# The bonus sums of an RWKV time mixing, tied to four steps of a block inverse's substitution

## The chip, the cores and the metric

The kernel runs on one core of a Trainium2 chip. A core has five engines that run side by side, each with its own fixed, in-order list of instructions: TensorE (PE, matmuls), VectorE (DVE), ScalarE (ACT), GpSimd (POOL) and SyncE (SP, which here only starts transfers). They wait for one another through semaphores. Transfers between the chip's memory (DRAM, HBM) and the core's buffers are issued from SP's, ACT's and POOL's lists and carried out by 16 DMA engines. The metric is device time in microseconds.

## The reference

One block of a streaming encoder, 512 frames of width 1024, in float32. A common in-projection feeds an RWKV-7 time mixing (8 heads of 64), a gated linear recurrence, and sigmoid gates that merge the two; then come a cross-attention into 256 memory frames and a gated convolutional feed-forward layer. What matters here:

```python
y = rwkv7_recurrence(r, decay, k, v, -kk, kk * a)
mean = jnp.mean(y, axis=-1, keepdims=True)
var = jnp.mean(jnp.square(y - mean), axis=-1, keepdims=True)
y = ((y - mean) * lax.rsqrt(var + LNX_EPS)).reshape(bsz, s, A_WIDTH) * lnx_g + lnx_b
bonus = jnp.sum(r * k * r_k, axis=-1, keepdims=True) * v
return (y + bonus.reshape(bsz, s, A_WIDTH)) * g
```

The bonus is a sum over a head's 64 channels for every frame, times v. It depends on r, k and v alone, and is needed only where y is normalised.

## The kernel before

**Layout.** Channels lie on the 128 partitions and frames along the free axis. A tile of 128x512 therefore holds two heads ("a pair", j = 0 to 3) for all frames. Matmuls keep float32 accuracy by splitting a float32 operand in a rounded high part (an ACT cast) and the remainder (a DVE subtraction), and summing two or three products. The sum over a head's channels, `sum_exact`, is such a product with a block matrix of ones: ACT casts the high part (L154), DVE makes the low part (L155), PE multiplies both (L156, L157).

**In-projection.** 38 column blocks of 24 matmuls each (three products, L160 to L162, by eight row blocks) go to the `in_ps` accumulators. Their weights are streamed: SP loads `win_r` (L102, four buffers), ACT casts it to `win_h` (L114), DVE makes `win_l` (L115); high and low parts have three buffers.

**Time mixing.** The pairs' stage lies between column blocks of the in-projection: `prep` and `prep2` build decays and scaled keys (tiles `AK`, `KBt`), with `ss` sums (also `sum_exact`) in between; `scores` does 16 small matmuls (L605), which DVE masks and evacuates to `BZ` and `AK` (L609, L610), and SP stores a part of `BZ` to DRAM, `dM` (L612). Then `bonus(j)` runs: DVE multiplies r, r_k and k (L586, tile `pr`), `sum_exact` sums them to `bo`, DVE multiplies by v (L589), ACT adds the bias (L590), and ACT's queue stores the result to DRAM, `dBo[j]` (L591).

**Block inverse.** All pairs' small matrices are loaded back from `dM` in one layout, `Nm` (L654, SP's queue). DVE inverts 128 triangular 32x32 blocks (two for each of 64 chunks of a head, one on each partition) by substitution: from s = 30 down to 0 a product (L660, tile `zz`) of (31-s) x (31-s) elements and a reduction (L661, tile `Zt`) of 31-s, so that the steps grow. The step s = 20 has an 11-element result. PE does gate blocks of the in-projection meanwhile, and ACT their sigmoids (L237, tile `gs`). The inverse goes through DRAM to `ZA`, the products `zh` and `zo` (L687, L695) use it, then come the chunk recurrence and `group_norm`, which loads `dBo` again (L821).

**What sets the order.** A scheduler fixes each engine's list when the kernel is built. The code's order counts unless a line has priority (weights, and the loads around the inverse) or is tied: `tc.issue_after(x)` puts what is inside it behind instruction x.

Of the kernel before, what the change touches and what calls it, by code (L numbers as in the profile page):

```python
# [9 lines left out]
F32 = mybir.dt.float32  # L10
F32R = mybir.dt.float32r
AF = mybir.ActivationFunctionType
ALU = mybir.AluOpType
AX = mybir.AxisListType
# [3 lines left out]
P = 128  # L18
T = 512
# [6 lines left out]
NPAIR = NH // 2  # L26
# [27 lines left out]
def hybrid_block_kernel(ctx: ExitStack, tc: tile.TileContext, xT_d, mT_d, pv_d, cst_d, win_d, wk_d, wv_d,  # L54
                        lup_d, gup_d, rga_d, rgx_d, wba_d, wbb_d, wmix_d, wq_d, wo_d, wfi_d, wfo_d, out_d):
    nc = tc.nc
    V, S, PE = nc.vector, nc.scalar, nc.tensor
# [12 lines left out]
    def mm_ps(name):  # L70
        return pmm.tile([P, T], F32, tag="mm", name=name)

    def rw_ps(name, pool=None, tag="rw", **kw):
        return (pool or prw).tile([P, T], F32, tag=tag, name=name, **kw)
# [9 lines left out]
    def par(name, i, n=1):  # L84
        o = PV[name][0]
        return pv[:, o + i:o + i + n]
# [63 lines left out]
    def sum_exact(ps, blocks, src, pool, tag, name):  # L150

        hi = pool.tile(list(src.shape), F32R, tag=tag, name=f"{name}_h", bufs=2)
        lo = pool.tile(list(src.shape), F32R, tag=tag, name=f"{name}_l", bufs=2)
        S.copy(hi, src)  # L154
        V.tensor_tensor(lo, src, hi.bitcast(F32), ALU.subtract)  # L155
        PE.matmul(ps, blocks, hi, start=True, stop=False)  # L156
        PE.matmul(ps, blocks, lo, start=False, stop=True)  # L157
# [36 lines left out]
    bonesr = cp.tile([P, P], F32R, name="bonesr")  # L194
# [72 lines left out]
    with tc.tile_pool(name="p0", bufs=1, reuse_waits="tile") as p0:  # L267
# [36 lines left out]
        for m in range(KB):  # L304
            ps = rw_ps(f"k_ps{m}") if 3 <= m < 6 else mm_ps(f"k_ps{m}")
# [93 lines left out]
    dBo = dr.tile([4, P, T], F32, name="dBo")  # L399
# [82 lines left out]
    vT = pa.tile([P, NPAIR, T], F32, name="vT")  # L482
# [4 lines left out]
    tp = tp_ctx.enter_context(tc.tile_pool(name="tp", bufs=1, reuse_waits="tile"))  # L487
# [28 lines left out]
    def inproj(i):  # L516
        ps = mm_ps(f"in_ps{i}")
        dense(ps, uin, lambda kb: (h2[:, 0, kb, :], h2[:, 1, kb, :]), KB, NSUM.get(i, 0))
        return ps

    def evac_shift(ps, blk, out):
        q = pp.tile([P, T], F32, tag="q", name=f"q{blk}", bufs=2)
        V.tensor_copy(q[:, 0:1], qb[:, blk:blk + 1])
        S.activation(q[:, 1:T], ps[:, 0:T - 1], AF.Identity, scale=par("mu", blk), bias=par("b_in", blk))
        V.scalar_tensor_tensor(out, ps, omu[:, blk:blk + 1], q, ALU.mult, ALU.add)  # L525
# [17 lines left out]
    def prep(j):  # L543
        sl = slice(j * P, (j + 1) * P)
        psw, psa = rw_ps(f"psw{j}"), rw_ps(f"psa{j}")
        for i, ps in enumerate((psw, psa)):
            PE.matmul(ps, lhi[:, i, sl], pwa[i], start=True, stop=False)
            PE.matmul(ps, llo[i][:, sl], pwa[i], start=False, stop=True)
        L = pp.tile([P, T], F32, tag="L", name=f"L{j}")
        tab(L, psw, AF.Sigmoid, bias=par("w0", j))  # L550
        at = pp.tile([P, T], F32, tag="at", name=f"at{j}")
        tab(at, psa, AF.Sigmoid, bias=par("a0", j))
        V.tensor_tensor_scan(L, smask, L, 0.0, ALU.mult, ALU.add)
        Pp = pp.tile([P, NC, HD + 1], F32, tag="Pp", name=f"Pp{j}")
        V.memset(Pp[:, :, 0:1], 1.0)
        tab(Pp[:, :, 1:], L.rearrange("p (c t) -> p c t", t=HD), AF.Exp, scale=-C0)
        tab(L, L, AF.Exp, scale=C0)
        V.tensor_copy(PC[:, j, :], Pp[:, :, HD])
        return at, L, Pp
# [22 lines left out]
            hs = half[e]  # L582
            V.tensor_tensor(AK[hs, e, jc, HD:P], c3(pr)[hs], Pp[hs, :, 1:], ALU.mult)

    def bonus(j, pk, pr):
        V.scalar_tensor_tensor(pr, pr, par("r_k", j), pk, ALU.mult, ALU.mult)  # L586
        ps = rw_ps(f"bo{j}")
        sum_exact(ps, bonesr, pr, tp, "xb", f"bo{j}")
        V.tensor_tensor(pr, ps, vT[:, j, :], ALU.mult)  # L589
        S.activation(pr, pr, AF.Identity, bias=par("lnx_b", j))  # L590
        nc.scalar.dma_start(dBo[j], pr)  # L591

# [3 lines left out]
    def scores(j):  # L598
        for e in range(2):
            hs, oh = half[e], half[1 - e]  # L600
            for cg in range(2):
                ps = rw_ps(f"sc{j}_{e}_{cg}")
                i0 = j * NC + cg * 4
                for i in range(4):
                    PE.matmul(ps[:, i * P:(i + 1) * P], kb_cols(j, e, cg * 4 + i), AK[hs, e, i0 + i, :],  # L605
                              start=True, stop=True)
                p3 = ps.rearrange("p (c t) -> p c t", t=P)
                m3 = scmask.unsqueeze(1).to_broadcast([P, 4, P])
                V.tensor_tensor(BZ[hs, i0:i0 + 4, :], p3[hs], m3[hs], ALU.mult)  # L609
                V.tensor_tensor(AK[oh, e, i0:i0 + 4, :], p3[oh], m3[oh], ALU.mult)  # L610
            with tc.high_priority(offset=1000000):
                nc.sync.dma_start(dM[e * 32 + j * NC:e * 32 + (j + 1) * NC].rearrange("i s t -> s i t"),  # L612
                                  BZ[hs, j * NC:(j + 1) * NC, 0:HD])

    def gate_block(b):
        ps = inproj(22 + b)
        sg = tp.tile([P, T], F32, tag="st", name=f"gs{b}", bufs=2)
        tab(sg, ps, AF.Sigmoid, bias=par("b_in", 22 + b))
        nc.scalar.dma_start(dG[b], sg)

    for jp in range(2):
        js = (2 * jp, 2 * jp + 1)
        pks, prs = {}, {}
        for j in js:
            pks[j] = pp.tile([P, T], F32, tag="pk", name=f"pk{j}", bufs=2)
            evac_shift(inproj(4 + j), 4 + j, pks[j])
        for j in js:
            prs[j] = pp.tile([P, T], F32, tag="pr", name=f"pr{j}", bufs=3)
            evac_shift(inproj(j), j, prs[j])
        for j in js:  # L630
            evac_shift(inproj(8 + j), 8 + j, vT[:, j, :])
        for j in js:
            if j == 3:
                for i in IN_REST[:NEARLY]:
                    gate_block(i - 22)
            at, L, Pp = prep(j)
            prep2(j, pks[j], prs[j], at, L, Pp)
            scores(j)
            bonus(j, pks[j], prs[j])

    pp_ctx.close()
    pq_ctx = ExitStack()
    pq = pq_ctx.enter_context(tc.tile_pool(name="pq", bufs=1, reuse_waits="tile"))
    YB = pq.tile([P, 4, T], F32, name="YB")


    with tc.tile_pool(name="pz", bufs=1, reuse_waits="tile") as pz:
        Nm = pz.tile([P, 32, 32], F32, name="Nm")
        Zt = pz.tile([P, 32, 32], F32, name="Zt")
        Zn = pz.tile([P, 32, 32], F32, name="Zn")  # L650
        zz = pz.tile([P, 31 * 31], F32, name="zz")
        with tc.high_priority(offset=1000000):
            for b in range(2):
                nc.sync.dma_start(Nm[b * HD:(b + 1) * HD], dM[:, b * 32:(b + 1) * 32, b * 32:(b + 1) * 32])  # L654
        V.memset(Zt, 0.0)
        V.memset(Zt.rearrange("p a b -> p (a b)")[:, 0:1024:33], 1.0)
        for s in range(30, -1, -1):
            n = 31 - s
            t3 = zz[:, 0:n * n].rearrange("p (a b) -> p a b", b=n)
            V.tensor_tensor(t3, Zt[:, s + 1:, s + 1:], Nm[:, s:s + 1, s + 1:].to_broadcast([P, n, n]), ALU.mult)  # L660
            V.tensor_reduce(Zt[:, s + 1:, s:s + 1], t3, AX.X, ALU.add)  # L661
        V.tensor_copy(Zn, Zt.rearrange("p a b -> p b a"))
        with tc.high_priority(offset=1000000):
            for b in range(2):
                nc.sync.dma_start(dZ[b], Zn[b * HD:(b + 1) * HD])
            nc.sync.dma_start(dZt, Zt[0:HD])
# [197 lines left out]
    def px_scan(b, xb, ga, gx):  # L864
# [5 lines left out]
        V.tensor_tensor(xb, xb, gx, ALU.mult)  # L870
        V.tensor_tensor_scan(YB[:, b, :], ga, xb, 0.0, ALU.mult, ALU.add)

    def py_block(b):
        ps = inproj(18 + b)
        ge = tp.tile([P, T], F32, tag="st", name=f"ge{b}", bufs=2)
        with tc.high_priority():
            tab(ge, ps, AF.Gelu_apprx_tanh, bias=par("b_in", 18 + b))
            V.tensor_tensor(YB[:, b, :], YB[:, b, :], ge, ALU.mult)

# [26 lines left out]
    for b in range(4):  # L906
        yb = YB[:, b, :]
        with tc.high_priority():
# [17 lines left out]
    for m in range(KB):  # L926
        ga = pm.tile([P, T], F32, tag="ga", name=f"gta{m}")
# [26 lines left out]
    for m in range(KB):  # L954
        xin = pm.tile([P, T], F32, tag="xin", name=f"xin{m}")
        nc.scalar.dma_start(xin, xT_d[:, m, :])
        ps = mm_ps(f"mix_ps{m}")
# [23 lines left out]
    pk = pk_ctx.enter_context(tc.tile_pool(name="pk", bufs=1, reuse_waits="tile"))  # L981
# [73 lines left out]
    pr = ctx.enter_context(tc.tile_pool(name="pr", bufs=1, side="right", reuse_waits="tile"))  # L1055
# [17 lines left out]
    for m in order:  # L1073
        ps = mm_ps(f"co_ps{m}")
# [87 lines left out]
    for m0 in range(0, FB, NQ):  # L1162
# [25 lines left out]
        for m in ms:  # L1188
            s = pc.tile([P, T], F32, tag="s", name=f"fs{m}")
# [228 lines left out]
```

## Time and profile before

| | us |
|---|---|
| runs | 909.81, 911.17, 912.35; median 911.17 |
| profiled execution, its own time | 909.73 |
| its span in the profile | 908.0 |
| PE busy | 890.5 (98%) |
| DVE busy | 687.4 (76%) |
| ACT busy | 510.4 (56%) |

The granted clock of PE was 0.998 on average. The profiled execution's span is what its instructions cover; 1.73 us of its time lie around it. A row of a timeline has the start, the duration, engine, line, operation, output and inputs, and in brackets how long the engine had idled just before and what ended it. A row of waits has the waiting instruction, what it waited for, the total in us, how often, and the longest. In the table of stretches the columns are the stretch, its length, and the busy time (and instructions) of PE, PE's weight loads, DVE, ACT and POOL, then the granted clock, the share of the DMA engines and GB/s.

### The profile page before, as it was taken

The numbers are of one execution on the slowest core, as the hardware profiler recorded it, in microseconds if no ns is written. First come the engines' busy times: TensorE is split into PE (matmuls) and PEld (weight loads), VectorE is DVE, ScalarE is ACT, GpSimd is POOL, SyncE is SP. The second block draws the span as 40 slices with busy tenths as digits, with TensorE's granted clock in tenths as the row PEclk, the third lists the DMA queues.
The fourth block names the chain that finished last, engine by engine and source line by source line (L and its number), as shares of the span: only waits on it lengthen the run. The fifth ranks groups of instructions, "written<-read, shape, count | busy, mean of one in ns | idle before, by whom it ended". The sixth has DMA issues, their size and how long they took to land. (4 is left out here: it accounts for less than half of the span.)

```text
span 908.0 us, 15914 instructions
## 1 busy us (share of the span) xinstructions
PE 890.5 (98%) x6218; PEld 776.1 (85%) x6218; DVE 687.4 (76%) x1096; ACT 510.4 (56%) x779; POOL 129.3 (14%) x159
## 2 busy tenths in 40 slices
PE   7999999999999999999999999999999999999996
PEld 6988877788877777887887778999999999999996
DVE  7884598776957585776565568788998888999674
ACT  6674675542236675234454446765665556767663
POOL 0102222010011212001112211111111111201100
PEclk9999999999999999999999999999999999999999
DMA  8878899667499749858788868898989998998963
GB/s 276 277 263 230 186 237 208 179 165 206 139 205 246 167 106 194 258 180 223 210 243 190 177 152 185 240 273 247 280 249 290 258 316 251 248 277 222 269 197 93
DMA packets 102411, 200.07 MB, mean 220 GB/s; under 512 B 25344, under 2 KB 36736, under 8 KB 102272
## 3 DMA queue, kind: packets, MB, share of 16 engines
q1 hardware_dynamic: 69504, 119.75, 41.0%
q0 software_dynamic: 25504, 67.38, 36.8%
q10 hardware_dynamic: 7328, 11.92, 3.9%
q8 instruction: 49, 0.80, 0.3%
q14 instruction: 26, 0.21, 0.1%
HBM read 187.75 MB, written 77.59 MB: 292 GB/s over the span
## 5 line engine op out<-in xcount | busy, mean ns | idle before, releaser
L126 ACT CAST wfi_h<-wfi_r 128x1024 fp32r<-128x1024 f32 x77 | 81.0, 1052 | 76.8 <-PE fx_ps L161 21.1
L160 PE MATMUL in_ps<-hT,win_h 128*128 128x512 f32 x304 | 121.9, 402 | 0.8 <-DVE pr L525 0.7
L162 PE MATMUL in_ps<-hT,win_l 128*128 128x512 f32 x304 | 120.8, 398 | 0.0
L161 PE MATMUL in_ps<-hT,win_h 128*128 128x512 f32 x304 | 120.6, 398 | 0.0
L127 DVE TENSOR_TENSOR wfi_l<-wfi_r,wfi_h 128x1024 fp32r<-128x1024 f32 x77 | 94.0, 1221 | 23.5 <-ACT wfi_h L126 23.3
L425 POOL DMA_DIRECT2D dS<-in_wfi x66 | 66.5, 1044 | 267.0 <-PE in_ps L160 132.4
L114 ACT CAST win_h<-win_r 128x1024 fp32r<-128x1024 f32 x38 | 39.8, 1048 | 71.9 <-PE in_ps L161 70.9
L115 DVE TENSOR_TENSOR win_l<-win_r,win_h 128x1024 fp32r<-128x1024 f32 x38 | 46.4, 1221 | 32.6 <-ACT win_h L114 32.5
L160 PEld LDWEIGHTS in_ps<-hT,win_h 128*128 128x128 f32 x304 | 57.0, 187 | 15.6 <-DVE pr L525 1.1
L161 PEld LDWEIGHTS in_ps<-hT,win_h 128*128 128x128 f32 x304 | 57.0, 188 | 14.0 <-issue 0.7
L162 PEld LDWEIGHTS in_ps<-hT,win_l 128*128 128x128 f32 x304 | 57.0, 187 | 13.9 <-issue 0.2
L461 POOL DMA_DIRECT2D dOs<-in_wfo x54 | 39.9, 804 | 186.0 <-PE fx_ps L160 50.9
L1245 DVE TENSOR_TENSOR wfo_l<-wfo_r,wfo_h 128x1024 fp32r<-128x1024 f32 (+1 forms) x39 | 47.2, 1210 | 13.6 <-ACT wfo_h L1244 13.5
L1244 ACT CAST wfo_h<-wfo_r 128x1024 fp32r<-128x1024 f32 (+1 forms) x39 | 40.4, 1038 | 28.2 <-PE oyz_ps L161 9.8
L161 PE MATMUL fx_ps<-hr,wfi_h 128*128 128x256 f32 x176 | 49.7, 282 | 0.0
L162 PE MATMUL fx_ps<-hr,wfi_l 128*128 128x256 f32 x176 | 49.7, 282 | 0.0
L160 PE MATMUL ox_ps<-go,wfo_h 128*128 128x256 f32 x176 | 49.6, 282 | 0.1
L160 PE MATMUL fyz_ps<-hq,wfi_h 128*128 128x256 f32 x176 | 49.3, 280 | 0.4 <-ACT p L1173 0.4
L160 PE MATMUL fx_ps<-hq,wfi_h 128*128 128x256 f32 x176 | 49.5, 281 | 0.0
L160 PE MATMUL fx_ps<-hr,wfi_h 128*128 128x256 f32 x176 | 49.4, 281 | 0.0
L162 PE MATMUL ox_ps<-go,wfo_l 128*128 128x256 f32 x176 | 49.3, 280 | 0.0
L161 PE MATMUL ox_ps<-go,wfo_h 128*128 128x256 f32 x176 | 49.3, 280 | 0.0
(418 smaller groups left out, 2727.8 us busy)
## 6 DMA issues: line engine op xcount, KB each, us to landing
dS<-in_wfi POOLq DMA_DIRECT2D x66, 512.0 KB, 8.4
wfi_r<-dS SPq DMA_DIRECT2D x44, 512.0 KB, 6.9
win_r<-in_win SPq DMA_DIRECT2D x38, 512.0 KB, 5.0
wfi_r<-in_wfi SPq DMA_DIRECT2D x33, 512.0 KB, 5.6
dS<-dS POOLq DMA_DIRECT2D x22, 512.0 KB, 5.7
dOs<-in_wfo POOLq DMA_DIRECT2D x12, 512.0 KB, 7.8
wv_r<-in_wv SPq DMA_DIRECT2D x8, 512.0 KB, 4.9
dG<-gs ACTq DMA_DIRECT2D x16, 256.0 KB, 2.6
```

What stands on the lines that cost most here:

```text
L114: S.copy(hi[:, o:o + n], raw[:, o:o + n])
L115: V.tensor_tensor(lo[:, o:o + n], raw[:, o:o + n], hi[:, o:o + n].bitcast(F32), ALU.subtract)
L126: S.copy(hi, raw)
L127: V.tensor_tensor(lo, raw, hi.bitcast(F32), ALU.subtract)
L160: first = PE.matmul(ps, lh, rh, start=start, stop=False, **kw)
L161: PE.matmul(ps, lh, rl, start=False, stop=False, **kw)
L162: PE.matmul(ps, ll, rh, start=False, stop=stop, **kw)
L425: return lambda: nc.gpsimd.dma_start(s(out), src, **kw)
L461: yield lambda k=k, w=w, src=src: nc.gpsimd.dma_start(dO[n, m][:, k * P:(k + w) * P], src, **kw)
L1244: S.copy(hi[:, :n], raw[:, :n])
L1245: V.tensor_tensor(lo[:, :n], raw[:, :n], hi[:, :n].bitcast(F32), ALU.subtract)
```

## The change

`bonus` is cut in two. `bonus_terms(j)` stays in the pair's place: it multiplies r, r_k and k and stores that product to DRAM, in `dBo[j]`. Ahead of the substitution four tiles `bt0` to `bt3` are allotted, and ACT's queue loads `dBo[j]` into them. The rest, `bonus(j, bt)`, is written into the substitution's loop and tied behind the reductions of s = 20, 16, 12 and 8 for j = 0, 1, 2 and 3. It overwrites `dBo[j]` with its result, as before. Computation is the same; four stores and four loads of 256 KB are added.

```diff
-    def bonus(j, pk, pr):
+    def bonus_terms(j, pk, pr):
+
         V.scalar_tensor_tensor(pr, pr, par("r_k", j), pk, ALU.mult, ALU.mult)
+        nc.scalar.dma_start(dBo[j], pr)
+
+    def bonus(j, bt):
         ps = rw_ps(f"bo{j}")
-        sum_exact(ps, bonesr, pr, tp, "xb", f"bo{j}")
-        V.tensor_tensor(pr, ps, vT[:, j, :], ALU.mult)
-        S.activation(pr, pr, AF.Identity, bias=par("lnx_b", j))
-        nc.scalar.dma_start(dBo[j], pr)
+        sum_exact(ps, bonesr, bt, tp, "xb", f"bo{j}")
+        V.tensor_tensor(bt, ps, vT[:, j, :], ALU.mult)
+        S.activation(bt, bt, AF.Identity, bias=par("lnx_b", j))
+        nc.scalar.dma_start(dBo[j], bt)
...
             scores(j)
-            bonus(j, pks[j], prs[j])
+            bonus_terms(j, pks[j], prs[j])
...
+    bts = [tp.tile([P, T], F32, tag=("ga", "gx")[j % 2], name=f"bt{j}", bufs=2) for j in range(NPAIR)]
+    for j in range(NPAIR):
+        nc.scalar.dma_start(bts[j], dBo[j])
...
-            V.tensor_reduce(Zt[:, s + 1:, s:s + 1], t3, AX.X, ALU.add)
+            ins = V.tensor_reduce(Zt[:, s + 1:, s:s + 1], t3, AX.X, ALU.add)
+            if s % 4 == 0 and 8 <= s <= 20:
+                with tc.issue_after(ins.ins):
+                    bonus(5 - s // 4, bts[5 - s // 4])
```

In the changed file `bonus_terms` has L587 and L588, the loads of `bt` L651, the substitution L667 and L668, the score evacuations L613 and L614, and the multiply by v L593. `sum_exact` keeps its lines.

**DVE, from the last score evacuation to the substitution.** Before, the bonus of pair 3 (L586, its low part L155, and the multiply by v, L589) lies between the evacuations and the first write of `Zt`:

```order
L610 TENSOR_TENSOR AK_746<-sc3_1_1_1718,cst_76 64x512
L586 SCALAR_TENSOR_TENSOR pr3_1354<-pr3_1354,pv_75,pk3_1278 128x512
L717 SCALAR_TENSOR_TENSOR cst_76<-cst_76 128x128 [waits DVE_49]
L115 TENSOR_TENSOR win_l22_2809<-win_r22_2806,win_h22_2808 128x1024 [waits DMAHW4_49,PE_49,Activation_49]
L155 TENSOR_TENSOR bo3_l_1729<-pr3_1354,bo3_h_1728 128x512 [waits Activation_49]
L589 TENSOR_TENSOR pr3_1354<-bo3_1727,vT_745 128x512 [waits PE_49]
L115 TENSOR_TENSOR win_l23_2843<-win_r23_2840,win_h23_2842 128x1024 [waits DMAHW7_49,PE_49,Activation_49]
L655 MEMSET Zt_1746 128x1024 [waits DMAHW1_49]
```

Now the product of pair 3 (L587) stands ahead of the score evacuations, and the low part of bonus 0 and its multiply stand inside the substitution:

```order
L667 TENSOR_TENSOR zz_1720<-Zt_1718,Nm_1717 128x121 [waits DVE_49]
L115 TENSOR_TENSOR win_l25_2923<-win_r25_2920,win_h25_2922 128x1024 [waits PE_49,Activation_49]
L668 TENSOR_REDUCE Zt_1718<-zz_1720 128x11 [waits DVE_49]
L155 TENSOR_TENSOR bo0_l_1749<-bt0_1706,bo0_h_1748 128x512 [waits DMAHW2_49]
L667 TENSOR_TENSOR zz_1720<-Zt_1718,Nm_1717 128x144 [waits DVE_49]
L668 TENSOR_REDUCE Zt_1718<-zz_1720 128x12 [waits DVE_49]
L667 TENSOR_TENSOR zz_1720<-Zt_1718,Nm_1717 128x169 [waits DVE_49]
L593 TENSOR_TENSOR bt0_1706<-bo0_1747,vT_745 128x512 [waits PE_49]
```

So the low part of bonus 0 comes after the reduction of s = 20, with one weight low part (win_l25) since the substitution's start.

**PE, the bonus products.** Before, both products of pair 3 stand in the column block in_ps28:

```order
L160 MATMUL in_ps28_2735<-hT2_0_89,win_h20_2738 128x512
L156 MATMUL bo3_1727<-bo3_h_1728,bonesr_80 128x512 [waits PE_49,Activation_49]
L161 MATMUL in_ps28_2735<-hT2_1_90,win_h20_2738 128x512
L162 MATMUL in_ps28_2735<-hT2_0_89,win_l20_2739 128x512
L160 MATMUL in_ps28_2735<-hT2_0_89,win_h20_2738 128x512
L161 MATMUL in_ps28_2735<-hT2_1_90,win_h20_2738 128x512
L162 MATMUL in_ps28_2735<-hT2_0_89,win_l20_2739 128x512
L157 MATMUL bo3_1727<-bo3_l_1729,bonesr_80 128x512 [waits DVE_49]
```

Now the first product of bonus 0 stands right behind the score matmuls of pair 3, and the second one 93 rows later, in in_ps31:

```order
L609 MATMUL sc3_1_1_1691<-AK_746,KBt_744 128x128 x3
L156 MATMUL bo0_1747<-bo0_h_1748,bonesr_80 128x512 [waits DVE_49,PE_49,Activation_49]
L160 MATMUL in_ps27_2712<-hT2_0_89,win_h19_2715 128x512
...
L160 MATMUL in_ps31_2851<-hT2_0_89,win_h23_2854 128x512
L161 MATMUL in_ps31_2851<-hT2_1_90,win_h23_2854 128x512
L157 MATMUL bo0_1747<-bo0_l_1749,bonesr_80 128x512 [waits DVE_49]
L162 MATMUL in_ps31_2851<-hT2_0_89,win_l23_2855 128x512
L156 MATMUL bo1_1765<-bo1_h_1766,bonesr_80 128x512 [waits PE_49,Activation_49]
```

Between the scores and L157 of bo0 stand 93 matmuls: the first bonus product, 6 of in_ps27, 72 of in_ps28 to in_ps30, and 14 of in_ps31. The products of bonus 1, 2 and 3 follow, their L157 17, 43 and 81 rows behind that of bonus 0.

**ACT, the cast win_h22 after pair 3's scores.** Before, it stands behind the store of a gate block and no transfer that waits for pair 3:

```order
L114 CAST win_h21_2773<-win_r21_2771 128x1024 [waits DMAHW1_49,PE_49]
L237 ACTIVATE gs4_2697<-in_ps26_2666,pv_75 128x512 [waits DMAHW0_49,PE_49]
L619 DMA dG_712<-gs4_2697 128x512 [waits Activation_49]
L114 CAST win_h22_2808<-win_r22_2806 128x1024 [waits DMAHW4_49,PE_49]
L154 CAST bo3_h_1728<-pr3_1354 128x512 [waits DVE_49]
```

Now pair 3's product is stored and loaded back ahead of it, and the load waits for the store (DMAHW0 is the semaphore of the store's landing):

```order
L237 ACTIVATE gs4_2709<-in_ps26_2678,pv_75 128x512 [waits DMAHW0_49,PE_49]
L623 DMA dG_712<-gs4_2709 128x512 [waits DMAHW7_49,Activation_49]
L588 DMA dBo_713<-pr3_1336 128x512 [waits DVE_49]
L651 DMA bt3_1709<-dBo_713 128x512 [waits DMAHW0_49]
L114 CAST win_h22_2820<-win_r22_2818 128x1024 [waits DMAHW6_49,PE_49]
```

What follows on win_h22 is win_l22 on DVE, then SP's load win_r26 (it needs the buffer), and behind that on SP the loads of Nm. The loads of bt1, bt0 and bt2 stand earlier on ACT: bt1 ahead of pair 2's squares, bt0 and bt2 ahead of the cast bo0_h and of pair 3's gates.

## The prediction

> **What bounds the kernel now.** I read the page first, then the waits of TensorE (PE), then the stretches of the span, and last the timelines of the four engines round the place where the work moves.
>
> The head of the page and its row of granted clock:
>
> ```profile
> span 908.0 us, 15914 instructions
> PE 890.5 (98%) x6218; PEld 776.1 (85%) x6218; DVE 687.4 (76%) x1096; ACT 510.4 (56%) x779; POOL 129.3 (14%) x159
> PEclk9999999999999999999999999999999999999999
> ```
>
> PE works 890.5 of 908.0 us at full clock. Every idle microsecond put into its stream is paid in full, and only 17.5 idle us are there to be won. PE's waits and the stretches say where these are:
>
> ```profile
> PE k_ps L160 <- ACT m L286: 6.2, 1, 6.2
> PE in_ps L160 <- DVE pr L525: 0.7, 1, 0.7
> PE bo L157 <- DVE bo_l L155: 0.6, 2, 0.4
> PE bo L156 <- DVE AK L610: 0.5, 1, 0.5
> PE in_ps L160 <- DVE pk L525: 0.2, 1, 0.2
> ...
> 100.00:150.00 50.00, 48.18 (x236) 38.00 (x235) 44.56 (x71) 33.86 (x45) 11.21 (x12) 1.00 0.92 208
> 150.00:200.00 50.00, 49.77 (x246) 40.15 (x245) 39.79 (x56) 27.77 (x37) 4.89 (x5) 1.00 0.67 175
> 200.00:250.00 50.00, 50.00 (x216) 40.18 (x215) 39.10 (x71) 14.73 (x18) 1.14 (x1) 1.00 0.62 180
> ...
> 903.00:904.00 1.00, 0.00 (x0) 0.00 (x0) 0.65 (x2) 0.00 (x0) 0.00 (x0) 0.77 1.01 283
> 904.00:908.00 4.00, 0.00 (x0) 0.00 (x0) 0.00 (x0) 0.00 (x0) 0.00 (x0) 0.50 0.62 178
> ```
>
> In each stretch the second number is PE's busy time; the clock is the third from the right. The pair loop (100 to 200) leaves 1.82 + 0.23 = 2.05 us idle; the substitution's stretch (200 to 250) leaves none. So the bonus costs PE little where it stands, and the question is what it meets where it goes.
>
> **The change part by part.** *Arithmetic.* Per pair the same product, cast, low part, two 128x512 matmuls, multiply and bias remain. Added are four 256 KB stores and four loads, 0.33 us of issue each on ScalarE's (ACT's) queue (first row of the second fence below), and ACT has long gaps (3.96 idle ahead of each cast there). This part is 0 on PE, except for what queues behind the loads, below.
>
> *The tie.* The second product of bo0 (L157) needs the low part that VectorE (DVE) writes after the reduction of step s = 20. The order of the changed kernel puts 93 matmuls on PE between the last score matmul of pair 3 and that product. I count everything from the first of those score matmuls:
>
> ```profile
> 187.75 3.68 PE L605 MATMUL sc<-AK,KBt 64*128 64x128 f32 x32
> ...
> 191.36 0.50 PE L160 MATMUL in_ps<-hT,win_h 128*128 128x512 f32 x1
> ```
>
> ```profile
> 199.97 0.33 ACTq L591 DMA_DIRECT2D dBo<-pr  x1
> ...
> 206.65 1.05 ACT L114 CAST win_h<-win_r 128x1024 fp32r<-128x1024 f32 x1 [3.96 <-PE in_ps L161]
> ...
> 212.25 1.05 ACT L114 CAST win_h<-win_r 128x1024 fp32r<-128x1024 f32 x1 [3.96 <-PE in_ps L161]
> ```
>
> The scores take 3.61 us. Two casts released by successive column blocks are 5.60 us apart, and a block has 24 matmuls, so one takes 0.2333. PE reaches the product at 3.61 + 93 x 0.2333 = 25.3 us. Now DVE and the load that starts the substitution:
>
> ```profile
> 189.30 0.68 DVE L609 TENSOR_TENSOR BZ<-sc,cst 64x512 f32<-64x512 f32 x1
> ...
> 194.80 0.73 DVE L586 SCALAR_TENSOR_TENSOR pr<-pr,pv,pk 128x512 f32<-128x512 f32 x1
> ...
> 196.01 1.23 DVE L115 TENSOR_TENSOR win_l<-win_r,win_h 128x1024 fp32r<-128x1024 f32 x1 [0.28 <-ACT win_h L114]
> 197.16 0.69 DVE L155 TENSOR_TENSOR bo_l<-pr,bo_h 128x512 fp32r<-128x512 f32 x1
> ...
> 212.45 0.16 DVE L660 TENSOR_TENSOR zz<-Zt,Nm 128x1 f32<-128x1 f32 x1 [3.22 <-DMA Nm<-dM]
> ...
> 215.07 1.22 DVE L115 TENSOR_TENSOR win_l<-win_r,win_h 128x1024 fp32r<-128x1024 f32 x1
> ...
> 218.42 0.28 DVE L661 TENSOR_REDUCE Zt<-zz 128x11 f32<-128x121 f32 x1
> ```
>
> ```profile
> 197.27 0.33 SPq L102 DMA_DIRECT2D win_r<-in_win  x1
> 197.78 8.65 SPq L654 DMA_DIRECT2D Nm<-dM  x2
> ```
>
> ```profile
> DMA to landing us min/median/max: 13.4/13.7/13.9
> ```
>
> The substitution waits for Nm, loaded after win_l22 has freed SyncE's queue (SP) at 197.24, and landing some 13.7 us after its issue (the last row, Nm's tile view). It starts at 212.45, that is 24.70. The 11-element reduction, s = 20, ends at 218.70, 6.25 later with one weight low part in between, as in the changed order. The bonus's low part adds 0.69: 31.64. PE comes at 25.3, the operand at 31.6: **PE stands still for 6.3 us**, and as PE is in order everything behind waits.
>
> *What moves the start.* The bonus product of pair 3 is now ahead of the score evacuations: up to +0.67. The load of bt3 waits for the landing of pair 3's own store, and win_h22 is behind it on ACT's queue; win_l22, win_r26 and Nm follow in turn. The landing rows are those of the tile views of pr (the store), dBo (stores and loads), and ZA (the nearest load of small blocks):
>
> ```profile
> DMA to landing us min/median/max: 2.0/5.4/6.7
> ...
> DMA to landing us min/median/max: 2.0/5.5/8.9
> ...
> DMA to landing us min/median/max: 5.5/7.3/9.3
> ```
>
> The product ends near 2.25; then 5.4 of landing, 0.33 issue, 1.05 cast and 1.23 low part give 10.3, against 9.49 before (197.24): +0.8; with the longest landing, 6.7, +2.1; with the shortest, DVE's own queue decides, 0. I take +0.5, as ACT's other waits can lie under it. Stall 6.8. Its bounds: Nm landing as ZA's loads do, 7.3 instead of 13.7, takes 6.4 off and leaves 0.4; the late landing gives 8.4.
>
> *What is won.* The waits named bo L157 (0.6, of which 0.35 precede 150 us), in_ps after pr (0.7) and after pk (0.2) fall away with the work that delayed DVE, about 1.4 together. The 0.5 ahead of bo's first product goes to the next user of the bank. Against it, the load of bt1 waits for its store ahead of pair 2's squares on ACT. At the median landing I put that at 0.5, so the net is -0.9; bounds -1.4 (no such wait) and +3 (an 8.9 landing, 3.4 above the median).
>
> *After the stall.* Bonuses 1 to 3 come 17 to 38 matmuls apart (4 to 9 us), near what DVE needs for its steps: +0.3, between 0 and 1.5. The substitution now has four low parts and four multiplies inside, 8 x 0.69 = 5.5 us. Its users:
>
> ```profile
> 253.11 1.12 DVE L662 COPY Zn<-Zt 128x1024 f32<-128x1024 f32 x1
> ...
> 266.45 1.19 PE L687 MATMUL zh<-ZA,BZ 32*32 32x32 f32 x32
> ```
>
> PE arrives there later by the 6.8 stall, so a delay of 5.5 + 0.5 is covered. Without the stall these 5.5 us would be exposed but for the slack of about 1 us there.
>
> *Clock.* A PE that stands still for 6.8 us may lose its clock. The two ends of the span show how:
>
> ```profile
> 6.20 0.58 PE L160 MATMUL k_ps<-m,wk_h 128*128 128x256 f32 x1 [6.20 <-ACT m L286]
> ...
> 12.60 0.42 PE L160 MATMUL k_ps<-m,wk_h 128*128 128x256 f32 x1
> ...
> 15.59 0.41 PE L160 MATMUL k_ps<-m,wk_h 128*128 128x256 f32 x1
> 15.81 0.40 PE L161 MATMUL k_ps<-m,wk_h 128*128 128x256 f32 x1
> ...
> 16.40 0.28 PE L162 MATMUL k_ps<-m,wk_l 128*128 128x256 f32 x1
> 16.52 0.28 PE L160 MATMUL k_ps<-m,wk_h 128*128 128x256 f32 x1
> ...
> 899.74 0.71 PE L1299 MATMUL rs_ps<-t,ones 128*128 128x128 f32 x4 [0.28 <-ACT t L1289]
> ```
>
> At the end PE stops at 900.45 and the clock falls within the window 903 to 904 (0.77, so near 903.5), some 3 us later. At the start the matmuls stand 0.22 apart until 15.8 and 0.12 after: 9.6 us at the low rate from the first, but only 3.2 from the last interruption at 12.6. While cold a microsecond does 0.117/0.213 = 0.55 of its work, so 3.2 to 9.6 us cost 1.4 to 4.3. The stream after the stall is dense, which is nearest the lower end; 4.5 us, so **+2.0**. Without the drop it is 0.
>
> [...]
>
> **Sum.** Stall 6.8, won -0.9, out of step 0.3, clock 2.0: +8.2. The profiled execution took 909.73 (span 908.0 and 1.73 round it), so 917.9; the three runs' median, 911.17, is 1.44 above that execution, within their own scatter. I say 918.0.
>
> **The rivals.** (1) *Stall without clock loss*: +6.2, 915.9. For it: the clock fell only 3 us after the last matmul, and the stall might be short enough or split by the partial products; against: 6.8 is twice that. (2) *Late landings on ACT*: the store of pair 1 ahead of bt1 and pair 2's sums, or bt0 ahead of bo0's cast and the gates of pair 3, lands as late as 8.9. Each is then 8.9 - 5.4 = 3.5 later than counted, and PE waits in the pair loop too: +2 to +6 on the forecast (one of them, less the idle that covers it, to both), 920 to 924. For it: the landings reach 8.9 in a loop whose DMA share is 0.92; against: their median is 5.4, and ACT is idle much of that time. (3) *Not slower*: Nm lands after some 7 us, since SP's second issue of it took 8.0 of the 8.65 us in its row, a queue that could be freer; the substitution then starts 6.4 earlier, the stall is 0.4 and no clock falls, so the 1.4 to 2.05 idle us of the pair loop are won: 908 to 910.5. It decides once Nm lands within 7 us of its issue. Against it: both landings stand at 13.4 to 13.9, with the same DRAM layout and the same neighbours on the queue. (4) *The low part is no wait at all* because the scheduler has put PE's product far enough behind; the order says 93 matmuls, so this goes with (3).
>
> **How the numbers follow.** The forecast has 0.55 (914 to 921: stall 4 to 8.4, clock 1.4 to 4.3), (1) 0.15, (2) 0.16, (3) with (4) 0.14. A measurement of this kernel tells about 0.3% (2.7 us) from no change. Slower is the forecast, (1) and (2), less a little for a short stall: 0.84. Case (3) falls within 0.3% for the greater part, 0.10, and beyond it when all 2.05 us and some of the scatter come together, 0.06. The range 911 to 924 leaves out most of (3), and the worst of (2) and of the clock.
>
> **What would show it.** In PE's waits of the changed kernel a row of bo L157 after DVE's bo_l, once, 6 to 7 us, near 213 us of the span; the rows of bo and pr in the pair loop smaller or gone; a clock below 1.00 in the 5 us behind the stall; Nm still landing 13 to 14 us after issue; zh without a wait. It is wrong if PE stays busy between 200 and 230, if the stall sits ahead of the sums or scores of pairs 2 and 3, or if the wait at zh is the largest.

## The result, and the profile after

The change takes 919.04 us (median of 7 runs, 917.15 to 921.15) against 911.17 before (7 runs, 907.84 to 916.45): a ratio of 1.0092, 95% interval 1.0073 to 1.0112. It is slower by 0.9%, about 8 us. The forecast was 918.0, slower. The profiled execution took 919.04, with a span of 917.3.

Page of the changed kernel, its head and the row of granted clock:

```profile
span 917.3 us, 15929 instructions
PE 890.5 (97%) x6218; PEld 775.5 (85%) x6218; DVE 686.9 (75%) x1096; ACT 511.0 (56%) x779; POOL 129.4 (14%) x159
```

PE's busy time is the same 890.5 us, so the 9.3 us that the span grew are idle time by this sum. Of these, 2.2 lie in the first 60 us (PE is busy for 51.08 us there instead of 53.32), ahead of everything that the change touches. A matmul at a low clock counts as busy for longer (0.63 us at 223.07 against 0.39 at 225.95, in the last timeline of this section), so the sum doesn't tell what the clock took. PE's waits in the changed kernel (waiting instruction, what it waited for, total, times, longest):

```profile
PE bo L157 <- DVE bo_l L155: 3.6, 1, 3.6
PE ss L156 <- ACT ss_h L154: 3.0, 1, 3.0
PE k_ps L162 <- DVE wk_l L115: 2.3, 2, 1.8
PE sc_ps L1026 <- ACT ex L1033: 1.2, 1, 1.2
```

The first is the wait that was forecast, but half its size. The second lies ahead of pair 2's sums: rival (2) had it, and the prediction named a stall at that place as a sign that it is wrong. The last two lie outside the change: at the very start of the span and in the cross-attention.

The stretches of the same kernel (PE's busy time is the second number, the clock the third from the right):

```profile
100.00:150.00 50.00, 48.80 (x240) 38.67 (x238) 42.59 (x67) 28.79 (x37) 11.23 (x12) 1.00 0.92 212
150.00:200.00 50.00, 46.82 (x226) 38.00 (x227) 36.80 (x52) 28.52 (x37) 4.90 (x5) 0.97 0.66 190
...
213.00:220.00 7.00, 5.24 (x23) 3.87 (x21) 4.37 (x22) 1.64 (x2) 0.00 (x0) 1.00 0.61 217
220.00:226.00 6.00, 4.17 (x11) 3.11 (x12) 5.79 (x14) 1.34 (x2) 0.00 (x0) 0.72 0.37 131
```

The pair loop (100 to 200) idles 4.38 us instead of 2.05. The stall at the bonus is idle time in both of the last two rows (1.76 + 1.83), and the clock behind it is down.

**The first wait.** The chain that ended last in the changed kernel, round pair 2's sums (start, us, what):

```profile
142.24 0.67 DVE pr L587
...
142.93 8.29 DMA dBo<-pr
...
151.25 0.33 ACTq L651
...
151.62 0.64 ACT sq L566
...
152.28 0.63 ACT ss_h L154
```

Pair 1's product is stored at 142.93 and takes 8.29 us to land. The load of bt1 waits for that on ACT, pair 2's squares stand behind the load, and PE waits for their sum. Nobody needs bt1 for another 70 us: its cast starts at 221.81.

**The second wait.** The chain again, then DVE and PE of the changed kernel at the place:

```profile
198.92 3.80 DMA dM<-BZ
...
202.79 0.60 SPq L661
...
203.44 11.42 DMA Nm<-dM
```

```profile
192.84 3.50 PE L609 MATMUL sc<-AK,KBt 64*128 64x128 f32 x32
...
214.94 0.16 DVE L667 TENSOR_TENSOR zz<-Zt,Nm 128x1 f32<-128x1 f32 x1 [3.46 <-DMA Nm<-dM]
...
219.77 1.22 DVE L115 TENSOR_TENSOR win_l<-win_r,win_h 128x1024 fp32r<-128x1024 f32 x1
220.90 0.27 DVE L668 TENSOR_REDUCE Zt<-zz 128x11 f32<-128x121 f32 x1
221.09 0.68 DVE L155 TENSOR_TENSOR bo_l<-bt,bo_h 128x512 fp32r<-128x512 f32 x1
...
221.83 0.50 PE L157 MATMUL bo<-bo_l,bonesr 128*128 128x512 f32 x1 [3.59 <-DVE bo_l L155]
...
223.07 0.63 PE L160 MATMUL in_ps<-hT,win_h 128*128 128x512 f32 x1
223.50 0.63 PE L161 MATMUL in_ps<-hT,win_h 128*128 128x512 f32 x1
...
225.95 0.39 PE L161 MATMUL in_ps<-hT,win_h 128*128 128x512 f32 x1
```

From the first score matmul of pair 3 PE comes to the product after 221.83 - 3.59 - 192.84 = 25.4 us (25.3 forecast). The substitution starts after 22.10 us (24.70 before, 25.2 forecast), the low part ends some 6.8 later, and PE stands 3.59 us. Behind it the matmuls are 0.43 us apart instead of 0.23 for some 3 us.

### The profile page after: what moved, and what is told of

It is laid out like the page before. It is cut to its first block, busy times and chain, and to the rows that moved or that the text cites. A ratio compares the mean times of both kernels' runs of the same rounds, so it can differ in the third digit from the quotient of the medians.

```text
span 917.3 us, 15929 instructions
## 1 busy us (share of the span) xinstructions
PE 890.5 (97%) x6218; PEld 775.5 (85%) x6218; DVE 686.9 (75%) x1096; ACT 511.0 (56%) x779; POOL 129.4 (14%) x159
## 4 chain that ended last, share of the span: by engine, by line
PE 86%; DVE 5%; DMA 5%; ACT 2%; issue 1%; SPq 0%; DVEq 0%; ACTq 0%
PE in_ps L160 6%; PE in_ps L162 6%; PE in_ps L161 6%; PE fx_ps L160 5%; PE fx_ps L162 5%; PE fx_ps L161 5%; PE fyz_ps L160 3%; PE fyz_ps L162 3%; PE fyz_ps L161 3%; PE ox_ps L160 2%; PE ox_ps L162 2%; PE ox_ps L161 2%; PE oyz_ps L161 2%; PE oyz_ps L162 2%; PE oyz_ps L160 2%; PE co_ps L160 2%
## 5 line engine op out<-in xcount | busy, mean ns | idle before, releaser
L126 ACT CAST wfi_h<-wfi_r 128x1024 fp32r<-128x1024 f32 x77 | 81.1, 1053 | 78.5 <-PE fyz_ps L161 25.5
L425 POOL DMA_DIRECT2D dS<-in_wfi x66 | 66.6, 1038 | 279.7 <-PE in_ps L160 149.8
L161 PEld LDWEIGHTS in_ps<-hT,win_h 128*128 128x128 f32 x304 | 57.7, 190 | 14.6 <-issue 1.0
L160 PE MATMUL fx_ps<-hq,wfi_h 128*128 128x256 f32 x176 | 49.8, 283 | 0.0
L160 PE MATMUL ox_ps<-go,wfo_h 128*128 128x256 f32 x176 | 49.7, 282 | 0.0
L160 PE MATMUL fyz_ps<-hq,wfi_h 128*128 128x256 f32 x176 | 49.4, 281 | 0.0
L161 PE MATMUL fx_ps<-hq,wfi_h 128*128 128x256 f32 x176 | 49.3, 280 | 0.0
L161 PE MATMUL fyz_ps<-hq,wfi_h 128*128 128x256 f32 x176 | 49.3, 280 | 0.0
```

The costliest lines, as they stand in the source:

```text
L126: S.copy(hi, raw)
L160: first = PE.matmul(ps, lh, rh, start=start, stop=False, **kw)
L161: PE.matmul(ps, lh, rl, start=False, stop=False, **kw)
L425: return lambda: nc.gpsimd.dma_start(s(out), src, **kw)
```

## The experiments

Each kernel is compared with the kernel before on the same chip. To see *where* time goes I also use PE's lag: the start of the same matmul of a column block on the timeline, minus its start in the profile of before, less that difference at the eighth column block (102.33 us before), which is only the scatter of the span's start. In the kernels with the tie seven of the eight bonus products, 7 x 0.2333 = 1.6 us of PE's work, come behind the 22nd block instead of ahead of it; there a lag of -1.6 after the pair loop is no gain. Theory A started as two separate stalls, each with its clock loss; after the first four runs it says in addition what sets the second one.

| run | median us | ratio to before (95%) | lag after pair loop (22 blocks) | lag after substitution's bonuses (31 blocks) |
|---|---|---|---|---|
| the change | 919.04 | 1.0092 (1.0073 to 1.0112) | +1.7 | +9.0 |
| e1 change again | 916.81 | 1.0075 (1.0048 to 1.0101) | +1.8 | +7.2 |
| e2 late loads | 920.05 | 1.0125 (1.0101 to 1.0149) | -3.4 | +6.3 |
| e3 no tie | 924.37 | 1.0165 (1.0148 to 1.0183) | +1.3 | +1.7 |
| e4 late loads, no tie | 915.10 | 1.0058 (1.0032 to 1.0085) | -2.1 | +6.4 |
| e5 quiet | 912.60 | 1.0028 (1.0002 to 1.0055) | +0.7 | +3.0 |
| e6 late loads, quiet | 913.95 | 1.0025 (1.0002 to 1.0048) | -3.4 | -1.3 |
| e7 before, quiet | 910.24 | 0.9991 (0.9970 to 1.0012) | 0.0 | 0.0 |
| e8 late loads, later steps | 921.36 | 1.0120 (1.0078 to 1.0161) | -3.4 | +8.3 |
| e9 loud | 924.84 | 1.0162 (1.0147 to 1.0177) | -0.5 | +12.1 |
| e10 late loads, no tie, quiet | 912.91 | 1.0029 (1.0011 to 1.0048) | -2.0 | -1.8 |
| e11 late loads, split, quiet | 914.82 | 1.0047 (1.0030 to 1.0064) | -1.3 | -1.3 |

**e1, the change again.**

> The change once more, as the yardstick of this set. Theory A (two separate stalls): PE waits about 3 us ahead of pair 2's sums (ss, behind the load of bt1 on ACT) and 3.6 us at bonus 0's second product, each followed by some 3 us at the low clock; in all +7 to +10 us on the kernel before. Rival B (the round trip and the moved work cost as such, spread over the span): the same sum, but PE's lag on the kernel before grows gradually and not at these two places.

+6.6 us by the medians, just below the expected +7. The two places are the same: 3.2 us ahead of pair 2's sums and 3.1 at bonus 0's second product. The lag jumps at them, from -2.7 to +3.3 between the 14th and the 15th column block and from +1.8 to +7.2 between the 23rd and the 28th, and grows nowhere else up to there: rival B, a cost spread over the span, falls for this part.

**e2, late loads.**

```diff
-        nc.scalar.dma_start(dBo[j], pr)
+        prst.append(nc.scalar.dma_start(dBo[j], pr))
...
-        nc.scalar.dma_start(bts[j], dBo[j])
+        with tc.issue_after(prst[-1].ins):
+            nc.scalar.dma_start(bts[j], dBo[j])
```

> The change, but the four loads of bt are issued only after the store of pair 3's product, so none stands ahead of pair 2's squares or pair 3's gates on ACT. Round trip, ties and work are those of the change. Theory A: the wait at ss (3.0) and its clock loss (1.4) go, the wait at bonus 0's second product stays at 2 to 5 us with its clock loss; +3 to +6 us on the kernel before, 4 less than the change. Rival B: +7 to +10, as the change, since as many bytes move.

The wait at ss is gone and the pair loop is 5.1 us faster than in the change (lag -3.4 against +1.7). But the time is no better, +9.8 us, outside what theory A expected (+3 to +6) and inside what rival B did (+7 to +10). Where it is lost speaks against B: the pair loop, in which the stores run, is faster, and the wait at the bonus is longer. That wait at the bonus, the landing of Nm by its tile view (minimum, median, maximum), and the timelines of PE, SP, GpSimd and DVE:

```profile
PE bo L157 <- DVE bo_l L155: 6.3, 1, 6.3
```

```profile
DMA to landing us min/median/max: 14.6/14.9/15.2
```

```profile
182.09 3.50 PE L611 MATMUL sc<-AK,KBt 64*128 64x128 f32 x32
...
190.94 5.55 SPq L664 DMA_DIRECT2D Nm<-dM  x2
...
190.98 1.16 POOL L425 DMA_DIRECT2D dS<-in_wfi  x1 [8.51 <-PE in_ps L160]
...
206.89 0.16 DVE L670 TENSOR_TENSOR zz<-Zt,Nm 128x1 f32<-128x1 f32 x1 [8.74 <-DMA Nm<-dM]
```

Nm now lands 15 us after its issue, not 7 to 11, and the stall has grown to 6.3, with the clock at 0.66 in the stretch from 210 to 220. So the two stalls are not independent. Two things had moved: the place of Nm among GpSimd's transfers, and the four loads of bt on ACT's queue, which now come shortly ahead of Nm. The first became the next question; e6 below tells it from the second.

**e3 and e4, no tie.** The four calls of `bonus` are written ahead of the substitution's loop and the tie is taken out; e4 has the late loads as well.

> The change without the tie: the four bonuses are written ahead of the substitution and go where the scheduler puts them (bonus 0's second product right behind the scores of pair 3, the others in the next 47 column matmuls). Round trip and early loads stay. Theory A: no wait of PE for bo_l in the substitution, the wait at ss stays with 2 to 4 us; +1.5 to +5 us on the kernel before. Rival C (the tie is harmless, its wait only takes up what would be waited for later at zh): +7 to +10 as the change, with a new wait at zh or behind it.

> Both undone: late loads and no tie; only the round trip through DRAM and the split remain. Theory A: neither stall, -1 to +2 us on the kernel before, no difference that can be measured. Rival B (round trip): +7 to +10.

Both came out worse than theory A said. In e3 (+14.1 us) the wait at the bonus is gone, as expected, but Nm lands 17 us after its issue and the products `zh` now wait for the inverse. PE's waits and Nm's landing in e3:

```profile
PE zh L696 <- DMA ZA<-dZt: 7.3, 1, 7.3
...
PE ss L156 <- ACT ss_h L154: 2.2, 1, 2.2
```

```profile
DMA to landing us min/median/max: 17.1/17.4/17.7
```

So part of rival C holds: here the late Nm is paid at `zh` instead of at the tie. In e4 there is no tie, and yet PE waits 5.9 us for a bonus low part. The profile of e4 on DVE:

```profile
208.06 0.16 DVE L672 TENSOR_TENSOR zz<-Zt,Nm 128x1 f32<-128x1 f32 x1 [6.12 <-DMA Nm<-dM]
...
209.31 0.68 DVE L155 TENSOR_TENSOR bo_l<-bt,bo_h 128x512 fp32r<-128x512 f32 x1
```

The scheduler has placed the substitution's first product, which waits 6.12 us for Nm, ahead of the last bonus's low part in DVE's list. That is the same wait as the tie's. The time of e4 is +4.9 us, and its ten runs spread from 909.18 to 920.75. The runs so far suggest one thing: what PE loses at the substitution hangs on when Nm lands. They don't show it by themselves, since other transfers and the order moved with it.

**Where Nm's landing comes from.** GpSimd starts 512 KB copies of weights from DRAM to DRAM (L425) behind the first matmuls of in_ps27, in_ps28 and in_ps29. GpSimd's timeline in the change, the second of them:

```profile
198.71 1.16 POOL L425 DMA_DIRECT2D dS<-in_wfi  x1 [8.74 <-PE in_ps L160]
```

Nm is issued 4.1 us later (its landings: 6.7 and 11.4); in e1 the gap is 4.0 (Nm landing 6.7 to 11.0). In before it is 2.1 (13.4 to 13.9), in e3 2.7 (17.1 to 17.7), in e2 0 (14.6 to 15.2) and in e4 0 (9.9 to 15.5). That gap alone doesn't put the landings in order: in e3 ACT's transfers take 25.5% of the DMA engines between 200 and 212 us, against 13.7% in the change. Five runs below move the copies and nothing else: e5 and e9 start from the change, e6 from e2, e7 from before and e10 from e4.

**e5, quiet, and e9, loud.** One table paces GpSimd's copies:

```diff
-            22: 2, 23: 1, 27: 1, 28: 1, 29: 1, 15: 4, ...
+            22: 2, 23: 1, 32: 1, 33: 1, 34: 1, 15: 4, ...      (quiet)
+            22: 2, 23: 1, 27: 1, 28: 3, 29: 2, 15: 4, ...      (loud)
```

> The change, with one number table altered: the three weight copies from DRAM to DRAM that GpSimd starts at the column blocks in_ps27 to in_ps29 (L425, 512 KB each) start at in_ps32 to in_ps34. Nothing else moves. So far Nm landed 6.7 to 11.4 us after its issue where the first copy had started 4 us earlier, and 10 to 17.7 where it started 0 to 3 us earlier. Theory A (these copies hold up Nm, and the stall at bonus 0's second product is Nm's landing less what the scheduler allowed): Nm lands in 5 to 9 us, the stall falls from 3.6 to between 0 and 2 us, with no clock loss behind it; the wait at ss (3 us) stays; +2 to +5 us on the kernel before. Rival D (Nm's many small pieces set its landing): landing and stall as before, +6 to +9.

> The opposite of the shift: in the change, GpSimd starts three weight copies in column block in_ps28 and two in in_ps29 instead of one in each, so that five instead of two stand round the load of Nm. Theory A (each copy that runs beside Nm puts off its landing): Nm lands in 13 to 20 us instead of 6.7 to 11.4, the stall at bonus 0's second product grows from 3.6 to 8 to 13 us, with one clock loss of about 2 us behind it as before; +13 to +19 us on the kernel before. Rival D (Nm's own pieces): stall 3 to 4 us, +6 to +9.

The stall disappears with the copies and grows with them. Of e5, Nm's landing, and the timelines with PE's scores and DVE's start:

```profile
DMA to landing us min/median/max: 5.8/7.2/8.6
```

```profile
191.32 3.50 PE L609 MATMUL sc<-AK,KBt 64*128 64x128 f32 x32
...
209.87 0.15 DVE L667 TENSOR_TENSOR zz<-Zt,Nm 128x1 f32<-128x1 f32 x1
```

There is no wait of L157 for a low part in e5; only the one at ss remains (2.0 us). The time is +1.9 us, just below what was expected (+2 to +5). Of e9, the wait, Nm's landing and the timelines; its time is +14.4 us:

```profile
PE bo L157 <- DVE bo_l L155: 8.0, 1, 8.0
```

```profile
DMA to landing us min/median/max: 14.8/15.3/15.8
```

```profile
190.38 3.50 PE L609 MATMUL sc<-AK,KBt 64*128 64x128 f32 x32
...
216.83 0.16 DVE L667 TENSOR_TENSOR zz<-Zt,Nm 128x1 f32<-128x1 f32 x1 [7.82 <-DMA Nm<-dM]
```

The queues' share of the 16 DMA engines between 200 and 212 us shows the rivalry. q0 carries GpSimd's copies, q1 SP's loads with Nm. The change, then e5 (which has no row of q0 there), then e9:

```profile
q0 software_dynamic: 535, 1.03, 49.3%
q1 hardware_dynamic: 3427, 1.01, 41.6%
```

```profile
q1 hardware_dynamic: 4455, 1.73, 73.3%
```

```profile
q0 software_dynamic: 759, 1.94, 73.3%
q1 hardware_dynamic: 922, 0.62, 18.9%
```

Where the copies run, SP's share falls, from 73.3% to 41.6% and 18.9%, and the later of Nm's loads lands after 8.6, 11.4 and 15.8 us. Rival D falls. And the stall follows from the start of the substitution. PE arrives 25.4 us after the first score matmul of pair 3, and DVE needs 6.9 from the start to the end of the low part, so a start later than 18.50 must be waited for. The start less 18.50 gives the stall to 0.02 us in the change (22.10: 3.59), in e1 (21.64: 3.14), in e9 (26.45: 7.95), and in e2 (24.80: 6.31); in e5 it is 18.55 and in e6 18.59, and there is none.

**e6, late loads and quiet; e7, the kernel before, quiet.**

> Late loads (no load of bt ahead of pair 2's squares) and the same shift of the three weight copies; the tie and the round trip stay as in the change. Theory A: neither stall, the pair loop's idle 1.8 us is won: -2 to +1 us on the kernel before. Rival D: as with late loads alone, a stall of 5 to 7 us, +6 to +11.

> The kernel before with the same shift of the three weight copies. Theory A: Nm lands 5 us earlier, but only DVE gains, as PE has no wait on the substitution: -0.5 to +0.5 us, no difference. Rival E (the copies' place changes the time by itself, whatever the bonus does): a change of over 3 us, which would make the two runs above unreadable.

e7 is no different from before (0.9991, 0.9970 to 1.0012): Nm lands after 5.4 to 7.6 us there, and PE gains nothing by it. Rival E falls. In e6 both stalls are gone, and up to the 31st column block PE is 1.3 us *ahead* of the kernel before, as theory A wanted. Nm lands after 8.1 to 9.0 us, so the late loads of bt explain little of the 15 us in e2. The whole is 1.0025, or +3.2 us by the medians, above the expected -2 to +1: in its profiled execution, the slowest of the ten, 3.2 us are waited for in the cross-attention, which comes 200 us later. More on that below.

**e8, later steps.** Late loads, and the tie at s = 14, 10, 6, 2.

> Late loads, and the tie at s = 14, 10, 6 and 2 instead of 20, 16, 12 and 8. The scheduler moves bonus 0's second product 25 column matmuls further back on PE (5.8 us), and by the trace of before the step s = 14 ends 6.0 us after s = 20. Theory A: the stall is the same as with late loads at s = 20, 4 to 7 us for a landing of Nm of 13 to 15 us, and with it the time, +5 to +11 on the kernel before. Rival F (a later step gives the operand time to come): stall below 2 us, time within 2 us of the kernel before.

PE's wait at the bonus in e8:

```profile
PE bo L157 <- DVE bo_l L155: 6.9, 1, 6.9
```

It is 6.9 us, with Nm landing after 14.5 to 15.6, against 6.3 in e2 with about the same landing; +10.7 us. Theory A holds, rival F falls: PE reaches the product 31.2 us after the scores instead of 25.4, so the scheduler has moved it back with the step, and a later step buys nothing. The step isn't at fault. By this the scheduler allows too little for the load that the steps wait for; its own reckoning is in no run.

**e10 and e11, what remains.** e10 is e4 with the quiet table. e11 has the late loads and the quiet table, and the tie holds only the multiply, the bias and the store:

```diff
+        bps = [bonus_sum(j, bts[j]) for j in range(NPAIR)]
         for s in range(30, -1, -1):
...
-                    bonus(5 - s // 4, bts[5 - s // 4])
+                    bonus(5 - s // 4, bts[5 - s // 4], bps[5 - s // 4])
```

> Late loads, no tie, and the three weight copies at in_ps32 to in_ps34: what remains of the change is the round trip through DRAM. DVE's last low part still stands behind the substitution's first product in its list, so that it waits for Nm. Theory A: with Nm landing in 5 to 9 us the stall of 5.9 us that the same kernel had without the shift goes: -2 to +1 us on the kernel before, and its runs no longer spread over 11 us. Rival B (the round trip costs as such): +4 or more.

> Late loads, the three weight copies at in_ps32 to in_ps34, and the bonus cut at another place: the four sums (cast, low part, both products of PE) are written ahead of the substitution, and only the multiply by v, the bias and the store are tied to s = 20, 16, 12 and 8. Theory A: PE waits for nothing of the tied steps, -2 to +1 us on the kernel before. Against it: the four accumulators stay taken until the multiplies, so a wait of PE for a bank may come in their place, +2 to +5.

In both no wait for a bonus is left (in e10 Nm lands after 8.1 to 8.5 us, in e4 it took 9.9 to 15.5), and after 31 blocks PE is 1.8 and 1.3 us ahead. e10's runs span 6 us (910.90 to 916.88) instead of e4's 11.6. No wait for an accumulator came in e11 either. Yet they are at 1.0029 and 1.0047, 2.5 and 4.4 us slower, more than expected. A wait of the cross-attention, in e10, and the landing of the reloaded keys, kvK:

```profile
PE sc_ps L1028 <- ACT ex L1035: 2.4, 1, 2.4
```

```profile
DMA to landing us min/median/max: 5.4/6.4/7.4
```

Just ahead ACT waits 4.9 us for these two loads; in before they landed after 4.3 and 5.2 us. The wait at sc_ps took 1.2 us in the change, 3.2 in e6, 1.3 to 2.4 in e8 to e11, 0.4 in e5 and e7, and none in e2, e3 and e4. What delays those loads was not tried. PE's lag tells at least where the rest is lost: at the 38th block it is -1.4 in e6, -0.9 in e10 and +0.8 in e11, at the last matmul +8.5, +2.3 and +3.3. So nearly all of it comes behind the in-projection. But e7, which has no round trip, goes from 0.0 to +3.2 there too in its profiled execution, the slowest of its ten, and single executions settle little. No version beats the kernel before. Whether the round trip costs the remaining 2 to 4 us or later transfers do stays open: rival B's +4 for e10 is neither shown nor excluded (+1.0 to +4.4 us).

## Why the prediction was right, and where its terms were not

**PE is the bound, and idle time is paid in full:** right. Busy time stayed at 890.5 us.

**The stall at bonus 0's second product:** right in place and cause, too large in size. PE's arrival at 25.3 us measured 25.4. The stall was put at 6.8 and measured 3.59 (3.14 in e1). The mis-sized term is the start of the substitution, taken as before's plus 0.5: Nm took 11.4 us to land, not 13.9. I had taken the landing over from before because Nm's neighbours on SP's queue were the same; the prediction says nothing of GpSimd's queue. That GpSimd's copies set the landing is shown by e5, e7 and e9; that it was earlier here because the copy beside it had started 4 us ahead instead of 2 fits the rows but was not tried. In e2, where Nm did take 15, the stall was 6.3. The chain also shows that Nm was released by the landing of the last dM store and not by the queue behind ACT's bt3 load, for which I had charged +0.5.

**What is won in the pair loop, -0.9:** wrong; it is the step that failed. I allowed 0.5 for bt1's load ahead of pair 2's squares, at a median landing of 5.4. The store of pair 1 took 8.29, near the longest of the rows I quoted, and PE waited 3.0 (3.2 in e1) with a clock loss behind. With the postponed products taken off, the loop is 1.7 + 1.6 = 3.3 us slower instead of 0.9 faster. The term's upper bound was +3, and rival (2) had the mechanism; by its own terms that bound is -0.9 + 3.4 = 2.5. Without that load in the way it would have been 3.4 - 1.6 = 1.8 faster (e2, e6, e8), somewhat more than the -1.4 that I took as the best.

**Clock, +2.0:** near in size for the one stall. Substitution and pair loop lost it both (0.72 from 220 to 226 us, 0.97 from 150 to 200). Between blocks 22 and 31 the change loses 7.3 us, of which 1.6 are postponed products and 3.6 the stall; 2.1 remain, the clock and what is out of step. In e5 and e6, which have no stall there and a clock of 0.996 over the whole span (0.993 in the change), 0.7 and 0.5 remain by the same sum, so my estimate of the clock's part is about 1.5. In the pair loop the clock's mean of 0.97 over 50 us (about 3 us with a matmul in 0.43 us instead of 0.23) is some 1.4 us more, which I had not counted as I expected no stall there.

**After the stall, +0.3, and zh covered:** right in the outcome. No row of waits has zh in the change, and PE waits for none of bonuses 1 to 3. Whether the stall covered the longer substitution, as I argued, is not shown. In e3, with no stall, zh waits 7.3, but the substitution also starts 27.8 us after the scores there instead of 22.1; in e5, with no stall and an early Nm, zh doesn't wait.

**Sum.** -0.9 + 6.8 + 0.3 + 2.0 = +8.2 against a measured +7.9 by the medians. That the two lie 0.3 apart is luck: the stall was 3.2 too large and the pair loop 4.2 too small. And from block 31 on some 2.4 us of the lag came back by block 38 (+6.6 there), and 1.2 went again in the cross-attention; I had forecast neither, and the first was not followed up.

**The rivals.** (1) without clock loss: no in the change, whose clock fell; but in e1 the stall of 3.14 us lost none. (2) late landings on ACT: yes for bt1, in addition to a smaller stall; bt0 and bt2 cost PE nothing. (3) not slower as Nm lands early: its mechanism is real, and e5 shows it (both loads landed by 8.6 us, no stall, 1.0028), but the point was set at 7 us, and what decides it is not SP's issue but GpSimd's copies.

## What to carry to other kernels

A tie to steps of a long chain puts the work behind that chain's *first* transfer; moving the tie to later steps does not help if the scheduler moves the consumer along, as it did in e8 (PE there 31.2 us after the scores instead of 25.4, stall 6.9). Before work is tied, look which transfers on other queues run beside the one it will wait for: here copies for a much later stage decided it, with none beside the load there was no stall, with two 3.1 to 6.3 us, with five 8.0. And a reload that nobody needs soon does not belong on a compute engine's queue ahead of work that is needed, for there it waits for its own store, 8.29 us here.

## What the runs showed of the hardware

Nm's two loads of 256 KB, in rows of 32 floats, landed 5.4 to 9.4 us after their issue in the five runs with the quiet table, and 6.7 to 17.7 beside GpSimd's 512 KB copies: up to three times as long, for the same bytes from the same queue.

In e1 the low clock came late. PE stood for 3.19 us until 151.94 and then ran six matmuls at full rate, 2.0 us, before the low rate began (PE's timeline of e1):

```profile
151.94 0.50 PE L156 MATMUL ss<-ss_h,bonesr 128*128 128x512 f32 x1 [3.19 <-ACT ss_h L154]
...
153.47 0.40 PE L162 MATMUL in_ps<-hT,win_l 128*128 128x512 f32 x1
...
154.34 0.63 PE L162 MATMUL in_ps<-hT,win_l 128*128 128x512 f32 x1
...
157.58 0.39 PE L161 MATMUL in_ps<-hT,win_h 128*128 128x512 f32 x1
```

It lasted from 153.94 to 157.32, 3.4 us. The other stall of the same execution, 3.14 us, was followed by no low rate at all (clock 1.00 from 219 to 230). In the change it began 1.4 us after the end of the 3.02 us at pair 2's sums, and 0.7 us after the end of the 3.59 at the bonus. After 7.95 us in e9 the first matmul was already slow (0.80 us, against 0.50 for the same one in the change), and in e2, with 6.31, the clock was 0.66 from 210 to 220. As a gap of 3.02 us was followed by the low rate and one of 3.14 was not, its length alone, by the modelled ends of the matmuls, doesn't decide it; what does, no run here settles.
